# The 288 contraction rows of an attention score packed into two full passes and 32-row products on separate quarters of the array

## The chip, the core and the metric

The kernel runs on one core of a Trainium2 chip. The core has a matrix engine (PE, with its weight loads shown as PEld), a vector engine (DVE), a scalar engine (ACT), a general engine (POOL) and a queue that mostly issues transfers (SP). The metric is the time of one execution on the device in microseconds (us). Lower is better.

## The reference

One transformer layer over 2048 tokens of width 1024, with 256 context tokens in front. A first norm and an input projection feed two branches: attention with 8 heads and a state-space recurrence. Then come an output projection, a norm, a gated feed-forward part and a last norm. All of it is held to float32 accuracy. The change concerns the scores of the attention alone:

```
scale = (QK_NOPE_DIM + QK_ROPE_DIM) ** -0.5          # 64 + 32 rows
s = einsum('bqhe,bkhe->bhqk', qn, k_nope) + einsum('bqhe,bke->bhqk', qr, k_rope)
p = softmax(s * scale)                               # over 256 + 2048 keys
o = einsum('bhqk,bkhe->bqhe', p, v)
```

Each head has its own 64 rows of keys without position (`k_nope`). The 32 rotated rows (`k_rope`) are the same for all heads.

## The kernel before, in words

**Accuracy.** A float32 operand is split into a high part, which one pass of the matrix engine carries, and a low part, which is the rest. A product of two operands is then three passes into the same accumulator: high by high, high by low, low by high. That is `mm3`, lines 61 to 65. `hi_of` (line 53) and `lo_of` (line 58) make the two parts, mostly on POOL.

**Stages.** Input projection, then queries, keys and values of all heads into scratch memory (`phase_qkv`), then attention, then gate, output projection and feed-forward part. The recurrence's input products end just before the attention starts. Its scan over chunks runs on POOL beside the first part of the attention (`scan_steps`, 8 steps per pair of query tiles, lines 774 to 776). Its read-out (`ReadOut`) follows: POOL splits the operands of a group of channels (`fetch`), and PE multiplies them (`issue`, two groups per pair).

**Attention.** The unit of work is a pair: one head and two tiles of 128 queries. There are 8 heads with 8 pairs each, 64 in all. For each tile, `op_S` computes the scores against 2304 keys in five blocks of 512, 512, 512, 512 and 256 columns. The first two blocks lie in the accumulator `SA`, the other three in `SB`. A block is one `mm3` over 96 rows (64 without position and 32 rotated), so a tile takes 15 passes. DVE takes the maximum (line 999), ACT the exponential (line 1010). PE then transposes the probabilities in groups of four (`tps`, line 1022), ACT and DVE split them (`pth`, `ptl`), and PE multiplies them with the values (`O`, lines 1045 and 1046). `SA` and `SB` have one buffer each.

**Order.** On PE, ACT, DVE and POOL the instructions are issued in the order of the program. A table (`ORDER`, or `ORDER_X` while the read-out runs) names the operations of one pair, with products and transposes of the pair before mixed in. After a pair's table, `ahead(i)` issues the splits of the queries of pair i+1 (`q_split`), the loads of pair i+2 (`q_load`) and, in some pairs of a head, the split of a third of the next head's keys (`k_split`) or a half of its values. The scan steps or a `fetch` of the read-out follow on POOL. In the read-out stage a second `fetch` stands in the middle of the table.

**Start of the attention.** The first head's keys are loaded straight into three free `PA` buffers (lines 1112 and 1113), ACT rounds them (line 1124), DVE takes the rest, and the first scores follow.

Of the kernel before, what the change touches and what calls it, by code (L numbers as in the profile page):

```python
# [24 lines left out]
DN = 64  # L25
# [58 lines left out]
def ln_stats(nc, sm, x, eps):  # L84
    """mean and 1/sqrt(var + eps) of each row of x."""
# [27 lines left out]
        # silu of both conditions and the bias of shift and scale, feature on partition  # L113
# [26 lines left out]
        # shift and scale of the first norm, for the latents and the context  # L140
# [11 lines left out]
        # input projection's weight, split  # L152
# [95 lines left out]
            # recurrent part, channel on partition, chunk position outermost and descending  # L248
# [51 lines left out]
        # the other four modulations of the latents, as rows  # L300
# [50 lines left out]
# --------------------------------------------------------------------------  # L351
# queries, keys, values of all heads
# --------------------------------------------------------------------------
def phase_qkv(tc, E, beside):
    """beside(n) issues n steps of the recurrence's input products."""
    nc = tc.nc
    I = E.I
    with ExitStack() as st:
# [4 lines left out]
        op.tile([128, 512], F32, name="qt1")  # L363
        for name in ("qt2", "qcos", "qsin"):
            op.tile([128, 512], F32, name=name, bufs=1)
# [30 lines left out]
        def rows(scr, i):  # L396
            """Two blocks of 128 rows, row of the block on partition."""
# [25 lines left out]
        def q_part(c, qh, ql, cos, sin):  # L423
# [15 lines left out]
            for m in range(2):  # L439
                p0 = qmm(4 + m)  # L440
                t1 = op.tile([128, 512], F32, name="qt1")
# [19 lines left out]
        for c in range(4):  # L461
# [5 lines left out]
            if c == 3:  # L467
                for p in range(2):
                    E.q0.append(load_q(nc, E, 0, p))
# [5 lines left out]
def load_q(nc, E, h, p):  # L475
    """Queries of a pair of tiles: without position, then rotated."""
    t = E.q_pool.tile([96, 256], F32, name="qraw")
    c, tok = p // 2, slice(p % 2 * 256, p % 2 * 256 + 256)
    nc.sync.dma_start(t[0:64], getattr(E, "qn_scr%d" % c)[h * 64:(h + 1) * 64, tok])
    nc.sync.dma_start(t[64:96], getattr(E, "qr_scr%d" % c)[h * 32:(h + 1) * 32, tok])  # L480
    return t


# --------------------------------------------------------------------------
# matrices of the recurrence, cut into chunks of CH tokens
# --------------------------------------------------------------------------
def s5_prep(tc, E, cp, wk, stage, up, ps_t, ps_p):
    """A generator: the eigenvalues first, then a group of channels per step."""
# [15 lines left out]
    # space that the first two groups of tokens take later  # L504
# [14 lines left out]
    # eigenvalues: state on partition (twice), (direction, group) free  # L519
# [13 lines left out]
    def exp(out, x):  # L533
        """exp at float32's accuracy: 2^k times a polynomial, the factor applied in two parts."""
# [42 lines left out]
    # powers 1..CH of the transition  # L577
# [13 lines left out]
    # input factor f = (a - 1) / lambda  # L591
# [24 lines left out]
        # the same without the power CH  # L616
# [3 lines left out]
    # scan table: [a8r, a8r ; a8i, -a8i] over (k, ri, direction, group pair), groups of a pair on the halves  # L620
# [9 lines left out]
    # B and C to state on partition  # L630
# [8 lines left out]
    for i in range(2):  # L639
        for half in range(2):  # L640
# [5 lines left out]
            # Y1 multiplies Re a^n, Y2 Im a^n; rows read (real state | imaginary state)  # L646
# [7 lines left out]
    # B bar, real over imaginary (X1) and its multiple by i (X2)  # L654
# [11 lines left out]
    # skip term  # L666
# [10 lines left out]
    def multiply(g):  # L677
        # input matrix by position in the chunk, descending: a^(CH-1-s) B forward, a^s B backward
# [5 lines left out]
        # read-out: C a^n  # L684
# [10 lines left out]
    def contract(g, w1, y1, yt):  # L695
# [6 lines left out]
        # impulse response within a chunk: a^0 .. a^(CH-1)  # L702
# [65 lines left out]
def scan_steps(tc, E, pool):  # L768
    """One chunk per step: state *= a^CH, plus what the chunk adds; both directions, all groups."""
# [10 lines left out]
def toeplitz(scr, g):  # L780
    """rows (position descending, channel), columns (position, channel) of the impulse response"""
# [5 lines left out]
class ReadOut:  # L787
    """Output of the recurrence, a group at a time."""
# [51 lines left out]
    def issue(self, now):  # L840
        """Products of one group; returns what finishes it, or None."""
# [49 lines left out]
def phase_attention(tc, E, inject):  # L891
    nc = tc.nc
    with ExitStack() as st:
# [9 lines left out]
        def head(h):  # L903
            if h not in heads:
                hd = Env()
                hd.raw = {}
                hd.kh = kp.tile([96, NTOK], F32R, name="kh")
                hd.kl = kp.tile([96, NTOK], F32R, name="kl")
# [6 lines left out]
        # loads run ahead of the splits that wait for them  # L915
        def k_load(h, c):
            raw = kp.tile([96, 768], F32, name="kraw", bufs=1)
            o = c * 768
            nc.sync.dma_start(raw[0:64, :], E.kT_scr[h * 64:(h + 1) * 64, o:o + 768])
            nc.sync.dma_start(raw[64:96, :], E.kr_scr[:, o:o + 768])  # L920
            head(h).raw["k", c] = raw

        def k_split(h, c):
# [4 lines left out]
            lo_of(P, hd.kl[:, sl], raw, hd.kh[:, sl])  # L928

        def v_load(h, c):  # L930
            raw = kp.tile([128, 9, 64], F32, name="vraw", bufs=1)
# [19 lines left out]
        def q_split(i):  # L951
            if i < NP:
                raw = qraw.pop(i)
# [4 lines left out]
                qs[i] = (qh, ql)  # L958

        def ahead(i):  # L960
            """Operands of the pairs to come, a little per pair."""
# [27 lines left out]
        def op_S(pr, j, c):  # L989
            S, o, w = ((SA, c * 512, 512) if c < 2 else (SB, (c - 2) * 512, min(512, KB - (c - 2) * 512)))  # L990
# [807 lines left out]
```

## Time and profile before

| | |
|---|---|
| median of 3 runs | 3342.23 us (3341.18 to 3343.07) |
| span of the profiled execution | 3336.3 us |
| PE busy | 3185.0 us, 95% |
| DVE, POOL, ACT busy | 1988.6, 1540.0, 1155.9 us |
| attention, first scores to last product | about 555 to 1560 us of the span |

The profile gives the span from the first to the last instruction of one execution. The median of the runs is 5.9 us longer, and this is what lies around the span. A busy PE is not a PE at its peak, because matrix products are pipelined: the distance from one start to the next is what a product costs in a stream. A wait shows as the idle time in front of an instruction, with the instruction that ended it.

### The profile page before, as it was taken

What the parts mean: (1) busy time and instruction counts of PE and PEld (TensorE: products, weight loads), DVE (VectorE), ACT (ScalarE), POOL (GpSimd) and SP (SyncE); (2) the same over time, 40 slices, a digit from 0 to 9 for tenths busy, and PEclk for the clock granted to TensorE, in tenths of its full rate; (3) what the DMA queues carried; (4) which work ended last, traced back from release to release, by engine and by line L of the source; (5) the groups of instructions that cost most, each with busy time, mean ns of one, the idle gap of its engine ahead of it and who ended that gap; (6) DMA issues with size and microseconds to landing.
All of it is one profiled execution on the core that took longest, in us unless ns stands there. A gap on an engine that the chain in (4) does not pass through costs nothing.

```text
span 3336.3 us, 46929 instructions
## 1 busy us (share of the span) xinstructions
PE 3185.0 (95%) x17221; PEld 2701.3 (81%) x17221; DVE 1988.6 (60%) x3233; ACT 1155.9 (35%) x2195; POOL 1540.0 (46%) x2206
## 2 busy tenths in 40 slices
PE   7899998999999999999878999999999999999998
PEld 4798877988988988988656788888888888888886
DVE  7855466888888777787389533354333633353337
ACT  2333354777777666676355300000010100010000
POOL 4765334877787999633344422233222422242223
PEclk9999998999999999999889999999999999999999
DMA  7543563111111222313866443334333433343324
GB/s 235 168 143 128 188 220 105 32 29 29 29 29 32 67 77 72 93 46 70 217 183 195 136 144 98 123 101 139 95 122 99 145 95 95 110 143 101 95 95 145
DMA packets 426486, 372.60 MB, mean 112 GB/s; under 512 B 91464, under 2 KB 354696, under 8 KB 426256
## 3 DMA queue, kind: packets, MB, share of 16 engines
q1 hardware_dynamic: 369248, 316.73, 31.9%
q10 hardware_dynamic: 57008, 52.87, 4.8%
q8 instruction: 136, 2.23, 0.3%
q14 instruction: 94, 0.77, 0.1%
HBM read 292.31 MB, written 77.22 MB: 111 GB/s over the span
## 4 chain that ended last, share of the span: by engine, by line
PE 62%; DVE 8%; POOL 7%; DMA 3%; issue 2%; ACT 1%; SPq 0%; POOLq 0%; DVEq 0%; ACTq 0%
PE pgu L65 9%; PE pgu L63 9%; PE pgu L64 9%; PE tps L1022 6%; PE pd L64 4%; PE pd L63 4%; PE pd L65 4%; PE O L1046 3%; PE O L1045 3%; PE SB L65 2%; PE SB L63 2%; PE SB L64 2%; POOL rhraw L53 2%; PE SA L64 1%; PE SA L63 1%
## 5 line engine op out<-in xcount | busy, mean ns | idle before, releaser
L53 POOL TENSOR_SCALAR whi<-wraw 128x1024 fp32r<-128x1024 f32 x275 | 302.7, 1101 | 1025.7 <-issue 339.2
L58 DVE TENSOR_TENSOR wlo<-wraw,whi 128x1024 fp32r<-128x1024 f32 x275 | 376.6, 1369 | 587.1 <-POOL whi L53 587.1
L65 PE MATMUL pgu<-u2h,wlo 128*128 128x512 f32 x1408 | 555.2, 394 | 2.0 <-DVE wlo L58 1.7
L63 PE MATMUL pgu<-u2h,whi 128*128 128x512 f32 x1408 | 552.1, 392 | 2.0 <-DVE hr L1582 1.0
L64 PE MATMUL pgu<-u2l,whi 128*128 128x512 f32 x1408 | 550.5, 391 | 1.9 <-DVE u2l L58 1.8
L1033 DVE TENSOR_TENSOR ptl<-tps,pth 128x512 fp32r<-128x512 f32 x576 | 380.1, 684 | 100.4 <-ACT pth L1027 100.1
L1027 ACT CAST pth<-tps 128x512 fp32r<-128x512 f32 x576 | 336.3, 586 | 162.7 <-PE tps L1022 138.6
L1580 ACT ACTIVATE sg<-pgu 128x512 f32<-128x512 f32 x88 | 52.6, 598 | 826.4 <-PE pgu L65 783.1
L1045 PE MATMUL O<-pth,vhl 128*128 128x256 f32 x1152 | 323.4, 304 | 0.6 <-DVE oo L1054 0.6
L64 PEld LDWEIGHTS pgu<-u2l,whi 128*128 128x128 f32 x1408 | 265.1, 188 | 63.9 <-DVE u2l L58 3.4
L65 PEld LDWEIGHTS pgu<-u2h,wlo 128*128 128x128 f32 x1408 | 265.2, 188 | 62.1 <-DVE wlo L58 4.6
L63 PEld LDWEIGHTS pgu<-u2h,whi 128*128 128x128 f32 x1408 | 265.1, 188 | 58.1 <-POOL u2h L53 1.4
L1046 PE MATMUL O<-ptl,vhl 128*128 128x256 f32 x1152 | 298.1, 283 | 2.2 <-DVE ptl L1033 2.1
L64 PE MATMUL pd<-wlo,hh 128*128 128x512 f32 x704 | 274.5, 390 | 2.2 <-DVE wlo L58 2.2
L63 PE MATMUL pd<-whi,hh 128*128 128x512 f32 x704 | 274.1, 389 | 0.0
L65 PE MATMUL pd<-whi,hl 128*128 128x512 f32 x704 | 274.0, 389 | 0.0
L999 DVE TENSOR_REDUCE mx<-SB 128x1 f32<-128x1280 f32 x128 | 190.6, 1489 | 78.2 <-PE SB L65 78.2
L1046 PEld LDWEIGHTS O<-ptl,vhl 128*128 128x128 f32 x1152 | 220.3, 191 | 10.1 <-DVE ptl L1033 3.3
L1045 PEld LDWEIGHTS O<-pth,vhl 128*128 128x128 f32 x1152 | 218.4, 190 | 7.8 <-ACT pth L1027 1.1
L1582 DVE TENSOR_TENSOR hr<-pgu,sg 128x512 f32<-128x512 f32 x88 | 60.6, 690 | 243.8 <-PE pgu L65 236.8
L1022 PE MATMUL tps<-ident,PB 128*128 128x128 f32 x1280 | 193.3, 273 | 4.6 <-DVE ptl L1033 4.6
L73 ACT ACTIVATE rq_s<-rq_v 128x1 f32<-128x1 f32 x68 | 12.5, 201 | 511.2 <-DVE rq_v L71 509.6
(439 smaller groups left out, 7299.1 us busy)
## 6 DMA issues: line engine op xcount, KB each, us to landing
wraw<-in_w_gate_up SPq DMA_DIRECT2D x176, 512.0 KB
wraw<-in_w_down SPq DMA_DIRECT2D x99, 512.0 KB
wad<-in_w_ada SPq DMA_DIRECT2D x32, 512.0 KB
wada<-in_w_ada SPq DMA_DIRECT2D x16, 512.0 KB
xt<-in_x SPq DMA_DIRECT2D x16, 512.0 KB
att_scr<-oo SPq DMA_DIRECT2D x64, 128.0 KB
ab<-att_scr SPq DMA_DIRECT2D x32, 256.0 KB
awb<-w_scr SPq DMA_DIRECT2D x64, 128.0 KB
```

Source lines behind the costliest of these rows:

```text
L53: eng.tensor_scalar(hi, raw, 1.0, 0.0, ALU.mult, ALU.add)
L58: eng.tensor_tensor(lo, raw, hi.bitcast(F32), ALU.subtract)
L63: nc.tensor.matmul(out, sh, mh, start=first, stop=False)
L64: nc.tensor.matmul(out, sh, ml, start=False, stop=False)
L65: return nc.tensor.matmul(out, sl, mh, start=False, stop=last)
L999: nc.vector.reduce_max(mx, SB if u else SA, axis=AX.X)
L1022: nc.tensor.transpose(ps[:, kk, j * 128:(j + 1) * 128], pr.P[(j, u)][:, o:o + 128], ident)
L1027: nc.scalar.copy(hi, pr.pt[g][0])
L1033: nc.vector.tensor_tensor(lo, ps, hi.bitcast(F32), ALU.subtract)
L1045: nc.tensor.matmul(o, vk, hi[:, kk, :], start=k in (0, 8), stop=False)
L1046: nc.tensor.matmul(o, vk, lo[:, kk, :], start=False, stop=k in (7, 17))
L1582: V.tensor_tensor(hr, pg[1], sg, ALU.mult)
```

## The change

The scores no longer use `mm3`. The three parts of the 96 rows make 288 rows: they are laid out as 128 + 128 + 32.

- The first pass multiplies `q1` (high and low part of the 64 rows, one above the other) with `kh` (the high part of the keys, twice).
- The second pass multiplies `q2` (high part of the 64 rows, high and low part of the 32 rotated rows) with `kl` (the low part of the keys, then twice the high part of the rotated keys). The lower half of `kl` doesn't depend on the head and is written once at the start, in two fixed buffers.
- The remaining 32 rows, the high part of the rotated queries by the low part of the rotated keys, are a product of 32 rows (`q3` by `kr3`). It is issued after block 1 for blocks 0 and 1, and after block 4 for blocks 2, 3 and 4. The products issued together stand on different quarters of the array's rows and write different banks.

A tile still issues 15 products: ten over 128 rows and five over 32. The operands are laid out anew for this. The queries are loaded twice (64 rows) and four times (32 rows), so a pair has six loads instead of two. Their split is now three POOL instructions and three ACT copies instead of two POOL instructions, and the last POOL instruction reads what an ACT copy wrote. To make room, several pools have one buffer instead of two, and the output of `op_OD` shares a tile with its input. At the start of the attention the `PA` and `PB` buffers first hold copies of the rotated keys.

```
-                qh = kp.tile([96, 256], F32R, name="qh")
-                ql = kp.tile([96, 256], F32R, name="ql")
-                hi_of(P, qh, raw)
-                lo_of(P, ql, raw, qh)
+                rn, rr = qraw.pop(i)
+                q1, q2, q3 = [kp.tile([128, 256], F32R, name="qs%d" % j) for j in range(3)]
+                hi_of(P, q1, rn)
+                lo_of(P, q1[64:128], rn[64:128], q1[64:128])
+                nc.scalar.copy(q2[0:64], rn[0:64])
+                nc.scalar.copy(q3, rr)
+                nc.scalar.copy(q2[64:96], rr[64:96])
+                lo_of(P, q2[96:128], rr[96:128], q3[96:128])
...
-            mm3(nc, S[:, o:o + w], qh[:, qo:qo + 128], ql[:, qo:qo + 128], hd.kh[:, ko:ko + w], hd.kl[:, ko:ko + w], True, True)
+            nc.tensor.matmul(S[:, o:o + w], q1[:, sl], hd.kh[:, c * 512:c * 512 + w], start=True, stop=False)
+            nc.tensor.matmul(S[:, o:o + w], q2[:, sl], hd.kl[:, c * 512:c * 512 + w], start=False, stop=False)
+            for e in {1: (0, 1), 4: (2, 3, 4)}.get(c, ()):
+                S, o, w = place(e)
+                rows = slice(e % 4 * 32, e % 4 * 32 + 32)
+                nc.tensor.matmul(S[:, o:o + w], q3[rows, sl], kr3[rows, e // 4 * 512:e // 4 * 512 + w], start=False, stop=True,
+                                 tile_position=(e % 4 * 32, 0))
...
+        for c in range(3):
+            raw = pp.tile([128, KA], F32, name="PA")[64:128, 0:768]
+            sl = slice(c * 768, (c + 1) * 768)
+            for j in range(2):
+                nc.scalar.dma_start(raw[j * 32:(j + 1) * 32], E.kr_scr[:, sl])
+            nc.scalar.copy(klr[0][64:128, sl], raw)
+            nc.vector.tensor_copy(klr[1][64:128, sl], raw)
+        raw = pp.tile([128, KB], F32, name="PB")[:, 0:768]
...
+            raw = pp.tile([128, KA], F32, name="PA")[:, 0:768]
+            for j in range(2):
+                nc.sync.dma_start(raw[j * 64:(j + 1) * 64, :], E.kT_scr[0:64, c * 768:(c + 1) * 768])
...
-            lo_of(P, hd.kl[:, sl], raw, hd.kh[:, sl])
+            lo_of(P, hd.kl[0:64, sl], raw[0:64], hd.kh[0:64, sl])
...
-            E.q_pool = E.q_st.enter_context(tc.tile_pool(name="q_raw", bufs=2, reuse_waits="tile"))
+            E.q_pool = E.q_st.enter_context(tc.tile_pool(name="q_raw", bufs=1, reuse_waits="tile"))
```

On PE this is the second pair's beginning, before the change: transposes (`tps`), the first block's three passes, transposes, the second block's three passes, products with the values (`O`).

```order
L1022 MATMUL tps<-ident,PA 128x128 x4
L63 MATMUL SA<-kh,qh 128x512
L64 MATMUL SA<-kl,qh 128x512
L65 MATMUL SA<-kh,ql 128x512
L1022 MATMUL tps<-ident,PA 128x128 x4
L63 MATMUL SA<-kh,qh 128x512
L64 MATMUL SA<-kl,qh 128x512
L65 MATMUL SA<-kh,ql 128x512
L1045 MATMUL O<-pth,vhl 128x256
```

The same place on PE in the changed kernel; `qs_6643`, `qs_6644` and `qs_6645` are `q1`, `q2` and `q3`, and `kr_6501` is `kr3`.

```order
L1036 MATMUL tps<-ident,PA 128x128 x4
L1002 MATMUL SA<-kh,qs_6643 128x512
L1003 MATMUL SA<-kl_6499,qs_6644 128x512
L1036 MATMUL tps<-ident,PA 128x128 x4
L1002 MATMUL SA<-kh,qs_6643 128x512
L1003 MATMUL SA<-kl_6499,qs_6644 128x512
L1008 MATMUL SA<-kr_6501,qs_6645 128x512 x2
L1059 MATMUL O<-pth,vhl 128x256
```

Each block has lost its third pass, and behind the second block stand two products on 32 rows each.

On POOL this is the end of a pair while the scan runs, before the change: the split of the queries between scan steps (`sct`, `hist`).

```order
L776 TENSOR_TENSOR hist<-hist,sct 128x64
L53 TENSOR_SCALAR qh<-qraw 96x256
L58 TENSOR_TENSOR ql<-qraw,qh 96x256
L774 TENSOR_TENSOR sct<-scan_tab,hist 128x128
L775 TENSOR_TENSOR hist<-hist,sct 128x64
```

The same place on POOL in the changed kernel.

```order
L777 TENSOR_TENSOR hist<-hist,sct 128x64
L53 TENSOR_SCALAR qs_6860<-qnraw 128x256
L58 TENSOR_TENSOR qs_6860<-qnraw,qs_6860 64x256
L58 TENSOR_TENSOR qs_6861<-qrraw,qs_6862 32x256
L775 TENSOR_TENSOR sct<-scan_tab,hist 128x128
L776 TENSOR_TENSOR hist<-hist,sct 128x64
```

One instruction has come in, and it reads `qs_6862` (`q3`), which ACT writes.

On ACT this is the end of a pair in the changed kernel: three copies between the last `pth` of the pair and the copy of `O`, where before `ot` followed `pth` directly.

```order
L1041 CAST pth<-tps 128x512 x2
L959 CAST qs_6861<-qnraw 64x256
L960 CAST qs_6862<-qrraw 128x256
L961 CAST qs_6861<-qrraw 32x256
L1064 COPY ot<-O 64x512
L1041 CAST pth<-tps 128x512
```

The copies that POOL's last instruction and PE's second pass wait for stand at the very end of the pair on ACT.

## Rows read from the trace of the kernel before

**Rows 1.** The page: busy time, share of the span and instructions of each engine.
```profile
PE 3185.0 (95%) x17221; PEld 2701.3 (81%) x17221; DVE 1988.6 (60%) x3233; ACT 1155.9 (35%) x2195; POOL 1540.0 (46%) x2206
```

**Rows 2.** Busy time by stretch: us, engines with instructions, clock, DMA share, GB/s.
```profile
555.00:1117.00 562.00, 553.28 (x3812) 503.11 (x3813) 462.51 (x700) 397.48 (x688) 434.32 (x1008) 0.99 0.12 32
1117.00:1370.00 253.00, 244.31 (x1730) 223.47 (x1730) 179.34 (x271) 161.55 (x292) 234.86 (x327) 0.99 0.26 75
```

**Rows 3.** The same stretches, only tile `ot`, written once per pair (DVE, ACT).
```profile
555.00:1117.00 562.00, 24.56 (x36) 20.98 (x36) 0.99 0.12 32
1117.00:1370.00 253.00, 10.24 (x15) 8.74 (x15) 0.99 0.26 75
```

**Rows 4.** Chain of waits over the attention: start us, us, what.
```profile
691.65 1.49 DVE mx L999
...
809.95 1.49 DVE mx L999
...
1100.01 3.90 DMA att_scr<-oo
...
1151.79 0.74 POOL ql L58
...
1168.28 0.74 POOL ql L58
...
1203.33 0.73 POOL ql L58
...
1222.46 0.72 POOL ql L58
```

**Rows 5.** Timeline of PE and its loads, one block: start us, us, instruction.
```profile
903.05 0.19 PEld L63 LDWEIGHTS SB<-kh,qh 96*128 96x128 f32 x1
903.08 0.48 PE L63 MATMUL SB<-kh,qh 96*128 96x512 f32 x1
903.16 0.19 PEld L64 LDWEIGHTS SB<-kl,qh 96*128 96x128 f32 x1
...
903.39 0.39 PE L64 MATMUL SB<-kl,qh 96*128 96x512 f32 x1
...
903.62 0.40 PE L65 MATMUL SB<-kh,ql 96*128 96x512 f32 x1
```

**Rows 6.** Timeline of PE in the input stage, small products (2*128, 64*64) between full ones.
```profile
42.32 0.66 PE L169 MATMUL pm<-ident,mrow 2*128 2x2 f32 x8
42.91 0.66 PE L191 MATMUL pt<-ident,xt 128*128 128x128 f32 x4
...
50.18 0.29 PE L65 MATMUL pkv<-wih,ul 128*128 128x288 f32 x1
50.40 0.66 PE L636 MATMUL pbt<-ident,sp_d 64*64 64x64 f32 x8
51.00 0.40 PE L63 MATMUL pkv<-wih,uh 128*128 128x288 f32 x1
51.24 0.29 PE L64 MATMUL pkv<-wil,uh 128*128 128x288 f32 x1
51.37 0.29 PE L65 MATMUL pkv<-wih,ul 128*128 128x288 f32 x1
```

**Rows 7.** Timeline of ACT and POOL at the end of a pair.
```profile
905.88 0.58 ACT L1027 CAST pth<-tps 128x512 fp32r<-128x512 f32 x1 [0.27 <-PE tps L1022]
...
907.34 0.40 POOL L53 TENSOR_SCALAR qh<-qraw 96x256 fp32r<-96x256 f32 x1 [1.45 <-PE SB L64]
...
907.82 0.73 POOL L58 TENSOR_TENSOR ql<-qraw,qh 96x256 fp32r<-96x256 f32 x1
...
908.36 0.58 ACT L1050 COPY ot<-O 64x512 f32<-64x512 f32 x1 [1.90 <-PE O L1046]
```

**Rows 8.** Timeline at the attention's start: the last copy before it, the first scores.
```profile
553.57 0.57 DVE L764 COPY hist<-px 64x255 f32<-64x255 f32 x1
...
554.97 0.77 PE L63 MATMUL SA<-kh,qh 96*128 96x512 f32 x1 [1.74 <-ACT kh L1124]
```

More of the change, by code (lines that the diff above doesn't have):

```diff
@@ L362, in phase_qkv @@
         ps = st.enter_context(tc.tile_pool(name="qk_p", bufs=5, space=PSUM, reuse_waits="tile"))
-        op.tile([128, 512], F32, name="qt1")
-        for name in ("qt2", "qcos", "qsin"):
+        for name in ("qt1", "qt2", "qcos", "qsin"):
             op.tile([128, 512], F32, name=name, bufs=1)
@@ L440, in q_part @@
                 p0 = qmm(4 + m)
-                t1 = op.tile([128, 512], F32, name="qt1")
+                t1 = op.tile([128, 512], F32, name="qt1", bufs=1)
                 nc.vector.tensor_tensor(t1, p0, cos, ALU.mult)
@@ L467, in phase_qkv @@
             if c == 3:
-                for p in range(2):
-                    E.q0.append(load_q(nc, E, 0, p))
+                E.q0.append(load_q(nc, E, 0, 0))
             q_part(c, qc[0], qc[1], cos, sin)
@@ L475, in load_q @@
 def load_q(nc, E, h, p):
-    t = E.q_pool.tile([96, 256], F32, name="qraw")
     c, tok = p // 2, slice(p % 2 * 256, p % 2 * 256 + 256)
-    nc.sync.dma_start(t[0:64], getattr(E, "qn_scr%d" % c)[h * 64:(h + 1) * 64, tok])
-    nc.sync.dma_start(t[64:96], getattr(E, "qr_scr%d" % c)[h * 32:(h + 1) * 32, tok])
-    return t
+    ts = []
+    for name, rows, scr in (("qnraw", DN, getattr(E, "qn_scr%d" % c)), ("qrraw", DR, getattr(E, "qr_scr%d" % c))):
+        t = E.q_pool.tile([128, 256], F32, name=name)
+        for j in range(128 // rows):
+            nc.sync.dma_start(t[j * rows:(j + 1) * rows], scr[h * rows:(h + 1) * rows, tok])
+        ts.append(t)
+    return ts
 def s5_prep(tc, E, cp, wk, stage, up, ps_t, ps_p):
@@ L906, in head @@
                 hd.raw = {}
-                hd.kh = kp.tile([96, NTOK], F32R, name="kh")
-                hd.kl = kp.tile([96, NTOK], F32R, name="kl")
+                hd.kh = kp.tile([128, NTOK], F32R, name="kh")
+                hd.kl = klr[h % 2]
                 hd.v = []
@@ L916, in k_load @@
         def k_load(h, c):
-            raw = kp.tile([96, 768], F32, name="kraw", bufs=1)
+            raw = kp.tile([128, 768], F32, name="kraw", tag="raw", bufs=1)
             o = c * 768
-            nc.sync.dma_start(raw[0:64, :], E.kT_scr[h * 64:(h + 1) * 64, o:o + 768])
-            nc.sync.dma_start(raw[64:96, :], E.kr_scr[:, o:o + 768])
+            for j in range(2):
+                nc.sync.dma_start(raw[j * 64:(j + 1) * 64, :], E.kT_scr[h * 64:(h + 1) * 64, o:o + 768])
             head(h).raw["k", c] = raw
@@ L927, in k_split @@
             hi_of(P, hd.kh[:, sl], raw)
-            lo_of(P, hd.kl[:, sl], raw, hd.kh[:, sl])
+            lo_of(P, hd.kl[0:64, sl], raw[0:64], hd.kh[0:64, sl])
         def v_load(h, c):
-            raw = kp.tile([128, 9, 64], F32, name="vraw", bufs=1)
+            raw = kp.tile([128, 768], F32, name="vraw", tag="raw", bufs=1)[:, 0:576].rearrange("p (t e) -> p t e", t=9)
             o = c * 9 * 128
@@ L989, in op_S, with place @@
         def op_S(pr, j, c):
-            S, o, w = ((SA, c * 512, 512) if c < 2 else (SB, (c - 2) * 512, min(512, KB - (c - 2) * 512)))
-            ko = c * 512
+            def place(c):
+                return (SA, c * 512, 512) if c < 2 else (SB, (c - 2) * 512, min(512, KB - (c - 2) * 512))
             hd = heads[pr.h]
-            qh, ql = qs[pr.h * 8 + pr.p]
-            qo = j * 128
-            mm3(nc, S[:, o:o + w], qh[:, qo:qo + 128], ql[:, qo:qo + 128], hd.kh[:, ko:ko + w], hd.kl[:, ko:ko + w], True, True)
+            q1, q2, q3 = qs[pr.h * 8 + pr.p]
+            sl = slice(j * 128, j * 128 + 128)
+            S, o, w = place(c)
+            nc.tensor.matmul(S[:, o:o + w], q1[:, sl], hd.kh[:, c * 512:c * 512 + w], start=True, stop=False)
[5 more added lines that the diff above has]
+                                 tile_position=(e % 4 * 32, 0))
         def op_M(pr, j, u):
@@ L1048, in op_OA @@
         def op_OA(pr):
-            pr.ot = sm.tile([64, 2, 256], F32, name="ot", bufs=1)
-            nc.scalar.copy(pr.ot, pr.O[64:128])
+            pr.ot = sm.tile([128, 2, 256], F32, name="ot", bufs=1)
+            nc.scalar.copy(pr.ot[0:64], pr.O[64:128])
         def op_OD(pr):
-            o = sm.tile([64, 2, 256], F32, name="oo", bufs=1)
-            nc.vector.tensor_tensor(o, pr.O[0:64], pr.ot, ALU.add)
+            o = pr.ot[64:128]
+            nc.vector.tensor_tensor(o, pr.O[0:64], pr.ot[0:64], ALU.add)
             nc.sync.dma_start(E.att_scr[:, pr.h * 64:(pr.h + 1) * 64, pr.p * 256:(pr.p + 1) * 256].rearrange("u e t -> e u t"), o)
@@ L1104, in op_XE @@
                 fills.pop(0)()
+        klr = [kp.tile([128, NTOK], F32R, name="kl%d" % j, bufs=1) for j in range(2)]
+        kr3 = kp.tile([128, 768], F32R, name="kr3", bufs=1)
+        for c in range(3):
[6 more added lines that the diff above has]
+        raw = pp.tile([128, KB], F32, name="PB")[:, 0:768]
+        for c in range(4):
+            nc.scalar.dma_start(raw[c * 32:(c + 1) * 32, 0:512], E.kr_scr[:, c * 512:(c + 1) * 512])
+        nc.scalar.dma_start(raw[0:32, 512:768], E.kr_scr[:, 2048:2304])
+        for r, o, w in ((128, 0, 512), (32, 512, 256)):
+            hi = pp.tile([128, KB], F32, name="PB").bitcast(F32R)[0:r, 0:w]
+            hi_of(P, hi, raw[0:r, o:o + w])
+            lo_of(nc.vector, kr3[0:r, o:o + w], raw[0:r, o:o + w], hi)
         qraw.update(enumerate(E.q0))
@@ L1110, in phase_attention @@
         for c in range(3):
-            raw = pp.tile([128, KA], F32, name="PA")[0:96, 0:768]
-            nc.sync.dma_start(raw[0:64, :], E.kT_scr[0:64, c * 768:(c + 1) * 768])
-            nc.scalar.dma_start(raw[64:96, :], E.kr_scr[:, c * 768:(c + 1) * 768])
+            raw = pp.tile([128, KA], F32, name="PA")[:, 0:768]
+            for j in range(2):
+                nc.sync.dma_start(raw[j * 64:(j + 1) * 64, :], E.kT_scr[0:64, c * 768:(c + 1) * 768])
             kraw.append(raw)
@@ L1119, in phase_attention @@
         q_split(0)
+        q_load(1)
         for _ in inject:
@@ L1124, in phase_attention @@
             nc.scalar.copy(hd.kh[:, sl], kraw[c])
-            lo_of(nc.vector, hd.kl[:, sl], kraw[c], hd.kh[:, sl])
+            lo_of(nc.vector, hd.kl[0:64, sl], kraw[c][0:64], hd.kh[0:64, sl])
         for c in range(2):
```

3 lines of the change are left out of this document (1 added, 2 removed).

## The prediction

> **What bounds the kernel now.** I read the page's busy times first: PE is busy 95% of the span [rows 1], but that is a mean over stages, and the change touches only the attention. So next the busy times by stretch [rows 2], with the count of pairs in each [rows 3]: 36 pairs end in the first stretch (scan beside the attention), 15 in the second (read-out beside it), and of the 64 the other 13 later. In the first, PE is busy 553.28 of 562 us. The maximum of the same place recurs 118.30 us later, 8 pairs on (691.65 to 809.95) [rows 4], so a pair takes 14.79 us. DVE needs 462.51 of 562 us there: 12.2 us of a pair at these clocks. In the second stretch the reader is to see another picture: POOL is busy 234.86 of 253 us with 327 instructions, and as it leaves about 0.08 us between two of them (0.40 from 907.34, next start 907.82 [rows 7]), 327 x 0.08 = 26 us more are taken. That is all of the stretch. The chain of waits says the same: there it runs through POOL's splits, `ql` to `ql` 16.49 us in a pair without a split of keys (1151.79 to 1168.28) and 19.13 us with one (1203.33 to 1222.46) [rows 4]. So PE sets the pace for about 49 pairs, POOL for most of 15.
>
> **PE, part by part.** In a stream a 512-column pass costs 0.235 us (903.39 to 903.62) [rows 5]; I take 0.12 for 256 columns, half of it (288 columns cost 0.13, 51.24 to 51.37 [rows 6]). A pair's scores before: 2 tiles x 3 x (4 x 0.235 + 0.12) = 6.36 us. After, the full passes: 2 x 2 x 1.06 = 4.24 us. If the 32-row products of a group truly run at once, a group costs one pass, 0.235: two groups per tile, 0.94 per pair, and the saving is 6.36 - 5.18 = 1.18 us per pair. If they run one after another, the five cost 2.12 and nothing is saved.
>
> Two things stand between. Each product has its own load of weights. The trace has a shape with few rows and 128 columns: eight loads with 2-row products in 0.59 us (42.32 to 42.91), at most 0.074 each with the way out, and I take 0.062 per load [rows 6]. The bound above is the like-typed load behind a break, 0.11 us (903.05 to 903.16) [rows 5]; the bound below is 0. So the second and third product of a group start 0.06 and 0.12 us late: groups of 0.30 and 0.36 us, 1.32 per pair (0.94 to 1.58).
>
> The other is the change between full and part array. [Rows 6] show it with 64-row products: the first starts 0.22 us after the full product in front of it, whose like follow each other at 0.13, so 0.09 is lost going in. From 50.18 to 51.24 there are 1.06 us, of which two full products are 0.26 and eight small ones at 0.06 to 0.074 are 0.48 to 0.59: 0.21 to 0.32 are lost in all, and I take 0.28. Where transposes follow I take 0.19, since after transposes the next pass pays the uncovered load in any case (903.08 to 903.39 is 0.08 more than a pass [rows 5]). A pair has four groups, by the table two in front of value products and two in front of transposes: 2 x 0.28 + 2 x 0.19 = 0.94 us per pair (0 to 1.28).
>
> The Trainium skill, on the page "TensorEngine Tiling (Array Packing)", Key Properties, says that switching the tiling mode, as against the tile, drains the engine. By that rule the loss per group is there whatever the neighbours; the trace agrees with it (0.22 us against 0.13). "TensorE: Matmul & The Clock Gate", Part 3, puts concurrent tiles about 4 ns apart; by that, groups would cost 0.24 us, 0.96 per pair, and PE's sum would be 0.22 us per pair lower than below. No row here shows products on different quarters together.
>
> Sum on PE: 4.24 + 1.32 + 0.94 = 6.50 against 6.36: +0.14 us per pair (between -1.18 and +1.28).
>
> **POOL.** The split of the queries grows by one subtraction over 256 columns, 0.73 us [rows 7], with its gap 0.81 us per pair; rows beside columns cost nothing, so the others keep their time. In the read-out stage POOL is the bound, and this goes straight onto the end: of 15 pairs I count 13, leaving one at either end to PE, 13 x 0.81 = +10.5 us (0 to 12). PE's +0.14 hides there. In the scan stage POOL has 562 - 434 - 1008 x 0.08 = 47 us left, 1.3 us per pair, but it used them by running nearly a pair ahead: at 907.34 it waited for the last scores of a pair just issued [rows 7]. Now its last subtraction waits for ACT's copy of `q3`, which ACT reaches only at the end of each pair. Queued behind it on POOL are key splits, scan steps and the next `q1`. The 515 us that POOL is taken there are 13.6 per pair, over the 38 pairs that 562 us hold. About 0.4 of this is the read-out's first two groups (16.49 us holds two), and about 1.5 the mean key and value split (three of 19.13 - 16.49 = 2.64 and two of values, taken a little smaller, over 8 pairs): 11.7 remain. A pair with a key split then needs 11.7 + 2.64 + 0.81 = 15.1, against 14.9 on PE: 0.2 us late, three times in each of 5 heads. I take +3 us for the stage (0 to 11).
>
> **ACT.** Three copies of 256 columns, about 0.4 us each (a cast of 512 columns takes 0.58 [rows 7]), stand where ACT idled 1.90 us in front of `ot` [rows 7]: hidden. From 906.46 they end at about 907.7, POOL's subtraction at about 908.0. `ot` starts at 908.36, behind the last value product, and PE still has four transposes and a pass to go before `q2`. That is about half a microsecond of cover; without it PE waits. SP's four more issues of about 0.5 us a pair, and the shared tile of `op_OD`, whose store takes 3.90 us [rows 4] of a 14.8 us pair, cost nothing.
>
> **Start.** Before, keys lay ready in `PA`, and the first scores followed the last copies at once (553.57, 554.97 [rows 8]). Now `PA` holds the rotated keys until ACT and DVE have copied them behind those same copies; then the keys' loads, then the rounding. For two of three thirds, which the second block needs: two more copies of about 0.8 us (768 columns, by the 0.58 for 512 [rows 7]), and one transfer of about 3.9 us [rows 4] behind them, and partly another in front. I take +8 us (3 to 14).
>
> **Sum**, from the profiled span of 3336.3 us, with the 5.9 us around it that the median has: scan 36 x 0.14 + 3 = 8.0; read-out 10.5; the last 13 pairs 1.8; start 8. Together +28: a span of 3364.6, a time of 3370.5, so 3371 us.
>
> **The rivals.** (1) *The packing pays.* The quarters run together, changing costs nearly nothing, and PE saves 1.18 us per pair. For it: PE bounds 49 pairs, and DVE's 12.2 leave room down to 13.6. Against it: the 0.22 us of [rows 6], and POOL. At most 49 x 1.18 = 58 less 3 of start: 3287. With POOL at 15.1 in three pairs of eight and a little less in two, the scan stage keeps only some 10 to 20 us, the read-out still costs 10 and the start 8; the tail gains 15. That makes about 3330, and less where POOL's extra is covered; I put 3322 as its time. (2) *It cancels.* PE gains 0.5 us per pair where it bounds (24 us), and POOL and the start take it: 3342. (3) *The quarters do not run together.* Five products in turn plus the changes: +0.94 per pair, 49 x 0.94 = 46, read-out 12, start 8: 3408. Against it: nothing in this trace, which has no such group; it decides from the point where a 32-row product starts 0.235 us after its neighbour.
>
> **How the numbers follow.** The forecast, slower by about 30 us, has 0.54, with its own range 3350 to 3395. Rival 1 has 0.18, rival 2 0.13, rival 3 0.15. The measurement can't tell less than 0.2%, 7 us, from no change. Faster takes rival 1: 0.18. Within takes rival 2: 0.13. Slower takes the forecast and rival 3: 0.69. The range for 8 in 10 is 3322 to 3412: it leaves out the lower half of rival 1 and the worst of rival 3.
>
> **What would show it.** Right: 32-row products in a group start 0.06 to 0.11 us apart, the first some 0.3 us behind its full pass, the next full one late; a pair near 14.9 us; in the read-out `ql`'s successors 0.8 us further apart than 16.49; first scores near 563. Wrong: a pair at 14.0 or less in the scan stage with POOL waiting there, or products of a group 0.235 us apart.

## The result, and the profile after

The changed kernel takes 3396.13 us (median of 4 runs, 3393.02 to 3398.78) against 3341.89 (4 runs, 3341.18 to 3343.07): 1.016 times as long, 95% interval 1.0146 to 1.0175. The forecast was 3371, with a range to 3412.

The page after: the span, and the row that answers to [rows 1]. (Of the 5.9 us by which the median of before exceeds its span, not all lies around the span: in every run with both on record the time is only about 2 us longer than the span. By that the profiled execution of before was a few us quicker than the median; the one of after was 2.7 us slower, so the two traces differ by 60 us and the medians by 54.)

```profile
span 3396.7 us, 48050 instructions
...
PE 3224.9 (95%) x17221; PEld 2633.8 (78%) x17221; DVE 2003.3 (59%) x3238; ACT 1233.3 (36%) x2390; POOL 1594.0 (47%) x2272
```

PE is busy 40 us longer with the same number of products, POOL 54 us. Where the time went is read from pair to pair, by the start of DVE's addition into `ot` (line 1054 of before, 1068 of after, 64 of them). All kernels of this study in us; the start is counted from the beginning of DVE's last copy into `hist` (553.57 in [rows 8], 556.63 after), since that copy begins anywhere between 551.9 and 557.3 from run to run, in kernels with the old scores (553.0 to 556.6) as in those with the new. "Usual pair" is the most frequent distance between two additions; one pair in eight is longer in every kernel (16.6 before, 16.8 after):

| kernel | start to first addition | 34 pairs of the scan | 17 of the read-out | last 12 | usual pair of the scan |
|---|---|---|---|---|---|
| before | 31.6 | 502.3 | 296.1 | 177.9 | 14.5 |
| after | 40.4 | 518.9 | 321.8 | 181.5 | 15.0 |
| e1 low part on DVE | 43.9 | 536.5 | 300.2 | 188.1 | 15.6 |
| e2 low part untied | 40.2 | 517.6 | 319.6 | 182.3 | 15.0 |
| e3 no keys at the start | 33.4 | 518.1 | 319.2 | 180.3 | 15.0 |
| e4 no 32-row products | 37.9 | 493.7 | 318.9 | 167.5 | 13.7 or 15.4 |
| e5 full third passes | 39.3 | 518.8 | 320.0 | 180.3 | 15.0 |
| e6 one quarter | 44.3 | 555.3 | 319.9 | 194.8 | 16.2 |
| e7 on DVE in read-out | 40.6 | 518.9 | 309.4 | 187.8 | 15.0 |
| e9 order | 41.6 | 511.9 | 319.2 | 179.1 | 14.8 |
| e10 full passes, order | 39.3 | 508.1 | 319.5 | 176.4 | 14.6 |
| e8 before, split off POOL | 31.8 | 502.6 | 292.1 | 188.5 | 14.5 |
| e11 before, POOL twice | 31.6 | 502.5 | 312.1 | 178.7 | 14.5 |
| e12 as e8, read-out only | 30.5 | 502.5 | 291.7 | 176.9 | 14.5 |

There is one trace per kernel. How well a stage repeats is seen where an edit leaves it alone: the scan took 502.3 to 502.6 in the four kernels with the old scan pairs and 518.1 to 518.9 in after, e3 and e7; the read-out took 318.9 to 320.0 in six kernels that keep POOL's work of after, which itself is the highest at 321.8. The kernel before, timed again beside the three sets of experiments, took 3339.5, 3345.0 and 3343.3, so a few us between sets say nothing by themselves.

From before to after the last addition comes 57.8 us later: 3.1 arise ahead of the attention, 8.8 at its start, 16.6 in the scan, 25.7 in the read-out, 3.6 in the last pairs. The busy times by stretch, which answer to [rows 2] (the third is the last pairs, behind it the same stretch of the kernel before):

```profile
565.00:1126.00 561.00, 551.14 (x3675) 443.12 (x3676) 458.71 (x682) 425.33 (x773) 440.09 (x1013) 0.99 0.16 42
1126.00:1420.00 294.00, 276.58 (x1852) 226.31 (x1850) 195.79 (x289) 193.81 (x361) 271.74 (x378) 0.97 0.29 80
1420.00:1621.00 201.00, 194.79 (x1304) 158.71 (x1303) 159.28 (x240) 148.50 (x270) 86.94 (x84) 0.98 0.23 62
...
1370.00:1563.00 193.00, 186.05 (x1290) 168.66 (x1289) 155.57 (x239) 135.11 (x235) 77.54 (x72) 0.99 0.19 54
```

In the first and the last PE leaves no more than 10 and 6 us, as before (9 and 7). In the second POOL is busy 271.74 of 294 us with 378 instructions, which leaves 0.06 us between two of them: no more than its usual gap.

The timeline of PE in an ordinary pair of the last stretch (start us, us, instruction), where POOL plays no part. The rows with L1008 are the groups of 32-row products:

```profile
1544.91 0.40 PE L1003 MATMUL SA<-kl,qs 128*128 128x512 f32 x1
1545.24 0.50 PE L1008 MATMUL SA<-kr,qs 32*128 32x512 f32 x2
1545.67 0.39 PE L1059 MATMUL O<-pth,vhl 128*128 128x256 f32 x1
1545.90 0.28 PE L1060 MATMUL O<-ptl,vhl 128*128 128x256 f32 x1
1546.02 0.28 PE L1059 MATMUL O<-pth,vhl 128*128 128x256 f32 x1
...
1547.62 0.28 PE L1059 MATMUL O<-pth,vhl 128*128 128x256 f32 x1
1547.85 0.38 PE L1060 MATMUL O<-ptl,vhl 128*128 128x256 f32 x1
1548.07 0.28 PE L1059 MATMUL O<-pth,vhl 128*128 128x256 f32 x1
1548.19 0.28 PE L1060 MATMUL O<-ptl,vhl 128*128 128x256 f32 x1
1548.30 0.28 PE L1002 MATMUL SB<-kh,qs 128*128 128x256 f32 x1
1548.42 0.28 PE L1003 MATMUL SB<-kl,qs 128*128 128x256 f32 x1
1548.63 0.50 PE L1008 MATMUL SB<-kr,qs 32*128 32x512 f32 x3
1549.06 0.66 PE L1036 MATMUL tps<-ident,PA 128*128 128x128 f32 x4
1549.48 0.47 PE L1002 MATMUL SA<-kh,qs 128*128 128x512 f32 x1
```

Three things are to be seen. A group of two and one of three take the same: one piece of 0.50, and 0.43 to the next start (1545.24 to 1545.67, 1548.63 to 1549.06). So the quarters run at once. But each group also costs time at its edges: it starts 0.33 after a 512-column pass that lasts 0.235 (1544.91 to 1545.24), the 0.43 are 0.195 more than a pass, and the value product behind it takes 0.23 instead of 0.12 (1545.67 to 1545.90); transposes behind it take 0.42 instead of 0.355. That is 0.39 or 0.35 us of array changes per group. And third, the value products at 1547.62, which no group touches (in the order table `V(1,1)`, the second batch of four of the pair before; `V(1,0)` is the first, at 1545.67), are 0.23 and 0.22 apart instead of 0.12. In the kernel before, the same products follow a 0.235 us pass each 0.12 apart:

```profile
1491.88 0.39 PE L65 MATMUL SB<-kh,ql 96*128 96x512 f32 x1
1492.11 0.28 PE L1045 MATMUL O<-pth,vhl 128*128 128x256 f32 x1
1492.23 0.28 PE L1046 MATMUL O<-ptl,vhl 128*128 128x256 f32 x1
1492.35 0.28 PE L1045 MATMUL O<-pth,vhl 128*128 128x256 f32 x1
```

What they wait for after is on DVE, whose timeline there is:

```profile
1545.78 1.23 DVE L1013 TENSOR_REDUCE mx<-SA 128x1 f32<-128x1024 f32 x1 [0.22 <-PE SA L1008]
1547.04 0.15 DVE L1018 TENSOR_SCALAR nm<-mx 128x1 f32<-128x1 f32 x1
1547.11 1.28 DVE L1047 TENSOR_TENSOR ptl<-tps,pth 128x512 fp32r<-128x512 f32 x2
```

The remainder `ptl` that V(1,1) multiplies stands behind the maximum of `SA`, and that waits for the group. The first of the two ends near 1547.75, half of the 1.28 us behind 1547.11. Between the end of `SA` and V(1,1) PE used to have the third passes of blocks 2 and 3 to do, 0.47 us; these now stand in the group behind block 4.

The chain of waits in the read-out, to be laid beside the `ql` rows of [rows 4]: POOL's last subtraction of the query split in each pair.

```profile
1154.72 0.73 POOL qs L58
...
1172.14 0.74 POOL qs L58
```

17.42 us apart in a pair without a key split, against 16.49. POOL also comes to this stage late. Its last scan step ends 9.9 us behind the start of the 35th addition (1125.85 to 1115.93); in the kernel before it ends 0.5 us behind it (1087.94 to 1087.45):

```profile
1115.93 0.69 DVE L1068 TENSOR_TENSOR ot<-O,ot 64x512 f32<-64x512 f32 x1
...
1125.53 0.32 POOL L777 TENSOR_TENSOR hist<-hist,sct 128x64 f32<-128x64 f32 x1
```

```profile
1087.45 0.68 DVE L1054 TENSOR_TENSOR oo<-O,ot 64x512 f32<-64x512 f32 x1
...
1087.62 0.32 POOL L776 TENSOR_TENSOR hist<-hist,sct 128x64 f32<-128x64 f32 x1
```

And at the start, where [rows 8] had the scores 1.4 us behind the last copy, the chain now is:

```profile
557.33 2.17 DMA PA<-kr_scr
...
559.53 3.50 DMA PB<-kr_scr
...
563.05 3.56 DMA PB<-kr_scr
...
566.68 0.85 POOL PB L53
...
567.90 0.95 DVE kl L58
...
568.98 0.76 PE SA L1003
```

The first pass of the scores starts at 565.54; the second waits until 568.98 for `kl`. On DVE `kl` stands behind the low part of `kr3` (`kr` in the rows), whose loads into `PB` (3.50 and 3.56 us, one behind the other) and whose rounding on POOL come last:

```profile
565.54 0.77 PE L1002 MATMUL SA<-kh,qs 128*128 128x512 f32 x1 [9.23 <-ACT kh L1158]
...
567.55 0.41 DVE L58 TENSOR_TENSOR kr<-PB 32x256 fp32r<-32x256 f32 x1 [0.29 <-POOL PB L53]
```

### The profile page after: what moved, and what is told of

It reads as the page before. It is cut to its first block, busy times and chain, and to the rows that moved or that the text cites. A ratio compares the mean times of both kernels' runs of the same rounds, so it can differ in the third digit from the quotient of the medians.

```text
span 3396.7 us, 48050 instructions
## 1 busy us (share of the span) xinstructions
PE 3224.9 (95%) x17221; PEld 2633.8 (78%) x17221; DVE 2003.3 (59%) x3238; ACT 1233.3 (36%) x2390; POOL 1594.0 (47%) x2272
## 4 chain that ended last, share of the span: by engine, by line
PE 53%; POOL 14%; DVE 8%; DMA 4%; issue 3%; ACT 1%; SPq 0%; POOLq 0%; ACTq 0%; DVEq 0%
PE pgu L64 9%; PE pgu L63 9%; PE pgu L65 9%; PE pd L64 4%; PE pd L65 4%; PE pd L63 4%; PE tps L1036 4%; PE O L1059 2%; PE O L1060 2%; POOL rhraw L53 2%; POOL sct L775 2%; PE SB L1002 1%; POOL qs L58 1%; PE SB L1003 1%; POOL rhl L58 1%
## 5 line engine op out<-in xcount | busy, mean ns | idle before, releaser
L1059 PE MATMUL O<-pth,vhl 128*128 128x256 f32 x1152 | 335.9, 313 | 0.6 <-DVE ot L1068 0.6
```

Of the source, the lines that this page charges most:

```text
L1059: nc.tensor.matmul(o, vk, hi[:, kk, :], start=k in (0, 8), stop=False)
```

## Experiments

The first four asked which of the costs is large: POOL's extra subtraction with its tie to ACT (A), the array changes (B), or the start (C).

**e1.**
```diff
-                lo_of(P, q2[96:128], rr[96:128], q3[96:128])
+                lo_of(nc.vector, q2[96:128], rr[96:128], q3[96:128])
```


> The low part of the rotated queries (rows 96 to 127 of q2, 256 columns per pair) is made on DVE instead of POOL; nothing else changes. Theory A (POOL's extra subtraction, and its wait for ACT's copy of q3, cost most outside the start; PE's own change is some 0.3 us per pair): the read-out stage loses the 0.9 us per pair by which POOL's queries stand further apart (17.42 to 16.49), about 13 pairs, and the scan stage the pairs of 15.5 to 17 us around key splits: 25 to 35 us, a time near 3366. Theory B (changing between full and part array costs most): POOL was not the limit, so under 8 us, near 3390. Theory C (the start costs most): under 8 us as well.

Measured: 3401.5 us, no gain where theory A expected some 30 us. The table shows why: the read-out does get 21.6 us shorter, but each pair of the scan grows from 15.0 to 15.6. The chain in that kernel, at the end of a pair:

```profile
640.85 0.46 PE SB L1008 x3
...
641.37 1.49 issue
642.85 0.43 DVE qs L58
643.29 0.14 issue
643.42 0.47 PE SA L1003
```

The 1.49 named "issue" are DVE's maximum of `SB` (start 641.33, 1.49 us). The subtraction stands behind it in the order of the program, and PE's second pass of the next pair waits for it. So A holds for the read-out; for the scan the run made a new wait and tells nothing.

**e2.**
```diff
-                lo_of(P, q2[96:128], rr[96:128], q3[96:128])
+                lo_of(P, q2[96:128], rr[96:128], q1[96:128])
```


> The subtraction stays on POOL but subtracts a tile that POOL itself made (q1's rows) in place of q3, which ACT makes; so it computes another value there and waits for no copy of ACT. Theory A: POOL can run ahead again; the scan stage's extra around key splits goes, 5 to 12 us, the read-out's 0.81 us per pair stays, near 3387. If POOL's busy time alone is what costs, nothing: 3396. Theories B and C: nothing, 3396.

Measured: 3397.7, no change. Without the tie the pairs of 15.4 in the scan, one in eight after, are 15.0 as well: the tie costs 1.2 us in 34 pairs. POOL now ends its last scan step 1.9 us behind the 35th addition instead of 9.9, so it is the tie that makes POOL late, and the first three pairs of the read-out take 49.6 us instead of 56.1 (before: 49.3). But the other 14 take 270.0 instead of 265.7, and the stage as a whole keeps 319.6. There the chain now has 4.2% in the loads of the read-out's matrices, which it had not, such as

```profile
1338.06 1.47 SPq L480
1340.31 2.16 DMA rmraw<-out_scr
```

where SP's queue, which also issues the queries' loads, stands in front of the load. That this queue limits where POOL's tie did is likely; no run takes the loads away.

**e3.**
```diff
-            for j in range(2):
-                nc.scalar.dma_start(raw[j * 32:(j + 1) * 32], E.kr_scr[:, sl])
-            nc.scalar.copy(klr[0][64:128, sl], raw)
-            nc.vector.tensor_copy(klr[1][64:128, sl], raw)
...
+        for j in range(2):
+            nc.gpsimd.memset(klr[j][64:128, :].bitcast(F32), 0.0)
+        nc.gpsimd.memset(kr3.bitcast(F32), 0.0)
```


> The rotated keys of all heads are not loaded, copied or rounded at the start; their tiles are filled with zeros by POOL instead (so the positional part of the scores is left out). Nothing else changes. Theories A and B: the first scores come 8 to 9 us earlier (573.43 to 561.60 less the 3.1 that arose ahead of it), near 3387. Theory C: 25 us or more.

Measured: 3389.7. The start falls from 40.4 to 33.4, 7.0 of the 8.8 us. C is out as the main cost.

**e4.**
```diff
-            nc.tensor.matmul(S[:, o:o + w], q2[:, sl], hd.kl[:, c * 512:c * 512 + w], start=False, stop=False)
+            nc.tensor.matmul(S[:, o:o + w], q2[:, sl], hd.kl[:, c * 512:c * 512 + w], start=False, stop=True)
...
-            for e in {1: (0, 1), 4: (2, 3, 4)}.get(c, ()):
+            for e in ():
```


> The 32-row products are left out (the low part of the rotated keys is missing from the scores); everything else stays, POOL's and ACT's work too. PE saves about 2.3 us per pair. Theory A: the read-out stage stays (POOL), the scan stage falls from 15.3 to the 14.4 to 14.7 us that POOL needs per pair, 20 to 30 us in all, and only the last 13 pairs gain in full or up to what DVE needs, 1.5 to 2.3 us each, 20 to 30 us: 3335 to 3355. Theory B: PE sets the pace nearly everywhere, 49 x 2.3 = 113 us less, near 3285.

Measured: 3355.5, at A's end and far from B's 3285. Of eight pairs of the scan three fall to 13.7, two stay at 15.4 behind POOL's key splits, where PE waits for POOL's `qs`, and the others lie between. The read-out does not move (318.9), so PE's groups play no part in its length. With all of the quarters' work gone the kernel is still 0.4% slower than before.

That left the 0.5 us per pair of the scan and the last pairs. The next four:

**e5.**
```diff
-                nc.tensor.matmul(S[:, o:o + w], q3[rows, sl], kr3[rows, e // 4 * 512:e // 4 * 512 + w], start=False, stop=True,
-                                 tile_position=(e % 4 * 32, 0))
+                nc.tensor.matmul(S[:, o:o + w], q3[:, sl], hd.kl[:, e * 512:e * 512 + w], start=False, stop=True)
```


> The 32-row products are replaced, at their places, by full 128-row passes over the same columns (with other values, so the scores differ): per tile two passes of 512 in the first group, two of 512 and one of 256 in the second, and no change between full and part array. All else stays. Theory A2 (packing costs PE 0.3 us per pair net: a group of two or three costs about 0.6 us whatever is in it, full passes 0.47 and 0.59; the further 0.2 us is a wait of the value products for DVE's remainder, made by the scores being shorter there): pairs of the scan stage go from 15.0 back to 14.5, so 34 x 0.5 = 17 us less there, 12 x 0.4 = 5 in the last pairs, nothing in the read-out stage, which POOL holds: near 3375. Rival (the 0.5 us per pair is ACT's and DVE's new load, not the array changes): scan pairs stay at 15.0, 3396.

Measured: 3397.5, pairs at 15.0: the rival's number. PE has no array change left here, and as many passes as the kernel before, yet a pair is 0.5 us longer. PE's timeline of an ordinary pair at V(1,0) and V(1,1):

```profile
917.72 0.27 PE L1058 MATMUL O<-pth,vhl 128*128 128x256 f32 x1
917.86 0.38 PE L1059 MATMUL O<-ptl,vhl 128*128 128x256 f32 x1
918.08 0.28 PE L1058 MATMUL O<-pth,vhl 128*128 128x256 f32 x1
...
919.67 0.28 PE L1058 MATMUL O<-pth,vhl 128*128 128x256 f32 x1
919.98 0.39 PE L1059 MATMUL O<-ptl,vhl 128*128 128x256 f32 x1
920.21 0.28 PE L1058 MATMUL O<-pth,vhl 128*128 128x256 f32 x1
```

V(1,1) now loses 0.30 us (0.31 and 0.23 in place of 0.12 each) and V(1,0) 0.12 (0.14 and 0.22), together twice the 0.21 of V(1,1) after: what PE saves it loses again in front of products with `ptl`. So the array changes and the wait had to be taken apart (e9, e10).

**e6.**
```diff
-                rows = slice(e % 4 * 32, e % 4 * 32 + 32)
+                rows = slice(0, 32)
```
(and `tile_position=(0, 0)`)

> All 32-row products use rows 0 to 31 of the array instead of one quarter each (and so the first block's keys in place of their own); number, columns and places stay. If the quarters ran truly at once in the changed kernel, a group of two now takes 0.235 us more and one of three 0.235 + 0.12: 1.18 us per pair, so 16.2 instead of 15.0 in the scan and the last pairs: 34 x 1.18 + 12 x 1.18 = 54 us, part of it again in the read-out, 3450 to 3470. If they had run one after another all along: no change, 3396.

Measured: 3455.4 (ratio to before 1.0315, 1.0299 to 1.0331), pairs at 16.2. A group of two reaches to the next start in 0.66 instead of 0.43:

```profile
911.64 0.73 PE L1008 MATMUL SA<-kr,qs 32*128 32x512 f32 x2
912.30 0.38 PE L1059 MATMUL O<-pth,vhl 128*128 128x256 f32 x1
```

The 1.18 us per pair that running at once was worth in the forecast are there in full.

**e7.** As e1, with `nc.vector if scanned else P`, so that the scan's pairs keep POOL.

> The low part of the rotated queries is made on DVE only in the pairs of the read-out stage; in the others POOL keeps it. Theory A2 (in the read-out POOL's extra subtraction and its tie to ACT's copy cost some 21 us; in the scan stage POOL is not the limit): 17 pairs of the read-out from 321.8 to about 300 us as in the run with DVE throughout, scan pairs at 15.0 as in the changed kernel: near 3375. If the gain there was paid for by the slower scan stage ahead of it: 3396.

Measured: 3393.1, little gain. The read-out falls by 12.4 us, not 21.6, and the last 12 pairs, where the subtraction is on DVE too, grow by 6.3 (15.6 each). Of the other 9 of e1's gain 5 lie at the entry: the first three pairs of the read-out take 55.2 us here and 50.1 in e1. Here POOL's last scan step ends 9.9 us behind the 35th addition, as after; in e1, where POOL has no low parts to make in the scan either, it ends 2.3 us ahead of it. The other 4 are spread over the pairs behind.

**e8.** The kernel before, its query split in the pairs behind the scan moved off POOL.
```diff
-                hi_of(P, qh, raw)
-                lo_of(P, ql, raw, qh)
+                if scanned:
+                    nc.scalar.copy(qh, raw)
+                else:
+                    hi_of(P, qh, raw)
+                lo_of(nc.vector if scanned else P, ql, raw, qh)
```


> The kernel before, with the split of the queries in the read-out pairs moved from POOL to ACT (high part) and DVE (low part); POOL is relieved of 0.40 + 0.73 us and two gaps, 1.3 us per pair. If POOL bounds that stage, its 17 pairs go from 296 us towards what PE needs (286 us busy): 5 to 15 us less, 3327 to 3337. If the low part waits on DVE behind the reduction of the second scores and PE waits for it: no gain or up to 5 us slower.

Measured: 3355.0, ratio 1.0025 (1.0016 to 1.0034): some 8 us slower, the second case of the expectation and more than its 5. The read-out gains 4.0 us, the last pairs lose 10.6, where PE's third pass, the one that reads `ql`, waits for DVE as its second pass did in e1 (9.0 us in 10 waits).

The last four test what remained: a wait at V(1,1) beside the array changes, and POOL alone.

**e9.** In the order table `S(0,0,4)` are the scores of this pair's first tile against block 4, with the group behind them.
```diff
-    ("S", 0, 0, 3), ("EA", 0, 0), ("L", 1, 2), ("V", 1, 1), ("S", 0, 0, 4), ("T", 1, 3),
+    ("S", 0, 0, 3), ("EA", 0, 0), ("L", 1, 2), ("S", 0, 0, 4), ("V", 1, 1), ("T", 1, 3),
```


> In the order of the scan stage and the last pairs, the value products V(1,1) are moved behind S(0,0,4) with its 32-row group; the read-out's order stays. Theory A3 (of the 0.5 us that a pair got longer, 0.2 is a wait of the second value product for DVE's remainder, which stands behind the maximum of SA: the third passes of two blocks used to lie in front of it): the wait goes, pairs of 15.0 become 14.8, 34 x 0.2 + 10 x 0.2 = 9 us, near 3387. Rival (PE's own changes are the whole 0.5): 15.0 stays.

Measured: 3387.1 (ratio to before 1.0137, 1.012 to 1.0154), pairs at 14.8, 9 us less than after: as expected. The trace agrees: 7.0 us less in the scan and 2.4 in the last pairs. V(1,1) no longer waits; only the array change shows at its first product:

```profile
1550.11 0.50 PE L1008 MATMUL SB<-kr,qs 32*128 32x512 f32 x3
1550.53 0.38 PE L1059 MATMUL O<-pth,vhl 128*128 128x256 f32 x1
1550.75 0.28 PE L1060 MATMUL O<-ptl,vhl 128*128 128x256 f32 x1
1550.87 0.28 PE L1059 MATMUL O<-pth,vhl 128*128 128x256 f32 x1
```

**e10.** The edits of e5 and e9 together.

> Full 128-row passes in place of the 32-row products (other scores) and V(1,1) behind S(0,0,4). With both gone, array changes and wait, theory A3 expects the pair of before, 14.5, less the part of POOL's lateness that then shows: scan 34 x 0.4 to 0.5 = 14 to 17 us less than the changed kernel, the last pairs 5 less, near 3377; and 0.3 us per pair less than the same order with quarters. That difference is the net price of the packing on PE. Rival (the pair is held at 15.0 by something else, since full passes alone left it there): 15.0.

Measured: 3380.2 (1.011, 1.0096 to 1.0123), pairs at 14.6. Full third passes in the new places are 0.2 us per pair quicker than the quarters; a loss of 0.13 is left, at V(1,0) as in e5. So packing two or three products per group costs PE more than not packing.

**e11.** The kernel before with one line of POOL twice.
```diff
                 lo_of(P, ql, raw, qh)
+                lo_of(P, ql, raw, qh)
```


> The kernel before, with the subtraction for the queries' low part made twice on POOL (the same result): POOL gets 0.73 + 0.08 us more per pair, as in the changed kernel, but with no tie to ACT, and PE is as before. If POOL's extra work is what costs in the read-out: 17 pairs x 0.81 = 14 us more there, up to 20 where POOL also arrives later at that stage; scan pairs stay at 14.5: near 3356. If the read-out's loss came from PE's array changes or from ACT: no change, 3342.

Measured: 3360.8, ratio 1.0048 (1.0035 to 1.006). The read-out grows by 16.1 us, the scan by 0.2. One subtraction of 256 columns gives 16 of the 25.7 us with nothing else changed. Of the 16.1 us 5.2 arise in the first three pairs of the stage; in the other 14 it costs 0.78 each, its 0.73 and a gap.

**e12.** As e8, under `if scanned and (ro.ready or ro.next < G)`, so that the last pairs keep POOL.

> The kernel before, with the split of the queries moved from POOL to ACT and DVE only while groups of the read-out are left, so that the last 12 pairs keep their 14.5 (with the split moved there too they took 10.6 us more). The read-out's gain of 4 us stays: near 3338, which is about what can be told from no change; if the pairs after it are late again, 3345 or more.

Measured: 3338.9, ratio to before 0.9985 (0.9976 to 0.9994): 4.4 us in the read-out, less than the 0.2% that can be told surely. It is the only kernel here that is not slower than before.

## Why the prediction came out as it did

The forecast, slower by PE's array changes, POOL's subtraction and the start, named the right mechanisms, but the loss was 54 us instead of 29: one term was missing and one too small. The time lies inside the stated range, but just outside the 3350 to 3395 that the forecast gave its own case, and nearer to rival 3's 3408 than to 3371. By the number alone one would have taken the wrong one of the two; e6 decides.

**PE, the full passes and the groups.** 4.24 us of full passes held. The groups and changes were put at 1.32 + 0.94 = 2.26; measured, with a group taken as one pass, are 4 x 0.235 = 0.94 for the groups and 2 x 0.39 + 2 x 0.35 = 1.48 for the changes, 2.42. The sum was near and its parts wrong: the 0.06 us of stagger per load, taken from eight small products in [rows 6], is not there (the products of a group start 3 to 4 ns apart in the trace), and the changes cost half as much again as the 0.28 and 0.19 taken. That the sum came near is luck. (Without stagger the prediction's own sum would have been 4.24 + 0.96 + 0.94 = 6.14, which is 0.36 below its 6.50; the 0.22 that it names for that case is the distance to the 6.36 of before.) The Trainium skill's "TensorEngine Tiling (Array Packing)", Key Properties, says that a switch of tiling mode drains the engine; the trace agrees, with 0.35 to 0.39 us per excursion. PE's balance is +0.30 us per pair instead of +0.14, confirmed by e9 (14.8 against 14.5), where the array changes are left alone.

**The term that was missing.** The other 0.2 us of the pair is the wait at V(1,1). The step that failed is the "Sum on PE": it adds passes, groups and changes, and has no term for what the moved passes had covered at their old places. Taking the third passes out of blocks 2 and 3 took away 0.47 us of PE work that covered DVE's maximum and remainder. e5 and e9 show it: without array changes the waits grow, and moving V(1,1) ends the one there. So the scan lost 16.6 us and not 8.0, and the last pairs 3.6 and not 1.8.

**POOL.** In the scan 3 us were put down for POOL's lateness; e2 shows 1.2 for the tie to ACT. That POOL holds the read-out and takes the subtraction in full was right, but 10.5 us became 25.7 (23 to 24 by the six like kernels). Of this e11 shows 16.1 for the subtraction alone. Pair by pair the forecast's 0.81 held (0.78 in e11); it was put on 13 pairs where the stage has 17, and the first three cost more. To this comes that POOL arrives late, with six scan steps still to do behind the 35th addition, and e2 shows that the tie does this. Yet e2 is no quicker over the whole stage. Taking the subtraction off POOL in the read-out only gives 12.4 back, in all pairs 21.6. How the other 9.6 divide between the late arrival, ACT's tie within the stage and SP's longer queue is not settled: e2 removed the tie and found loads late instead.

**Start.** +8 was forecast, 8.8 measured, 7.0 of it by the rotated keys (e3). The size was right and the path only in part: the prediction summed copies out of `PA`, the keys' loads and their rounding, and on that path the first pass came at 565.5. What ended last was the path of `kr3` through `PB`, POOL and DVE, for which it had no term; that the sum fits so well is luck. **ACT's copies** cost nothing that a run shows.

**The rivals.** That the quarters do not run at once is out (e6). That packing pays fails on PE's array changes, ahead of POOL: e10's plain passes beat it. It could not have paid in this kernel even with groups that cost nothing: e4 leaves them out, and the read-out and the start still keep it at 3355.5. That it cancels is out by the interval.

**The signs named beforehand.** First scores: near 563 was said; they come at 565.5, 3.1 of it from ahead. The pair: near 14.9 was said, from a mean of 14.79 over eight pairs; the like mean after is 15.28, while the usual pair grew from 14.5 to 15.0. POOL's subtractions in the read-out: 0.8 further apart was said, 0.93 measured in the pair shown. Products of a group 0.06 to 0.11 apart: wrong, they start together. The sign against it, 0.235 apart, is not seen either.

## What to carry to other kernels

Count an excursion from the full array to part of it as a price of its own, here 0.35 to 0.39 us, whether it holds two products or three: two 512-column passes saved (0.47 us for 0.62) don't pay it; three full ones in one group (0.70) would, by an estimate from the same rows that no run here tests. When passes are gathered behind a later block, look at what they covered at their old places: the next engine's chain may have been just in time. And where an engine fills a stage with its work and its gaps, each added instruction lengthens the stage in full, while moving that instruction to an engine with room helps only if it doesn't queue there behind something that is itself awaited.

## What was not expected of the hardware

Products of 32 rows on different quarters show as one piece of 0.50 us for two and for three; the loads of their weights don't stagger them. The same subtraction of 32 rows by 256 columns takes 0.73 us on POOL and 0.43 on DVE. One such subtraction added on POOL cost 0.78 us in each of the later pairs of the read-out, its 0.73 us and a gap, but 5.2 us more in the first three (e11).
